# Joint small instructions in a token-major norm, gates spread differently, and sums of logarithms as fp32r products, in a two-block transformer kernel

## The chip, the cores and the metric

The kernel runs on one core of one Trainium2 chip. The metric is device time in microseconds (us) from launch to end, the median of three runs. One further execution was recorded by the hardware profiler; its trace is what the prediction is argued from. Engines are named as in the profile: PE (matrix products), PEld (its weight loads), DVE (vector), ACT (scalar), POOL (GpSimd), SP (which here only issues DMAs).

## The reference, cut to what matters

A first block (four mixers, a feed-forward layer with squared ReLU, a gated per-layer embedding) is followed by two DeepNorm layers. Layer 0 is dilated attention and a sparse mixture of 16 experts, layer 1 is stick-breaking attention and the same kind of mixture. There are 256 tokens of 1024 features, all in float32. The parts that the change touches:

```python
def rmsnorm(x, g):                 # before the feed-forward layer, the gates and the dilated attention
    y = x32 * lax.rsqrt(jnp.mean(x32 * x32, axis=-1, keepdims=True) + EPS)

def layer_norm(x, g, b):           # after each mixture: x = layer_norm(ALPHA * x + ffn, ...)
    mu = xf.mean(-1, keepdims=True)
    var = jnp.square(xf - mu).mean(-1, keepdims=True)
    return ((xf - mu) * lax.rsqrt(var + LN_EPS) * g + b).astype(x.dtype)

# stick-breaking attention, per head; z is the clipped score
sp = jnp.where(strict, jnp.log1p(jnp.exp(z)), 0.0)      # the logarithms
r_in = jnp.einsum('bhnqj,js->bhnqs', sp, suffix)        # their sums from key j on
att = jnp.where(strict, jnp.exp(z - r_in), 0.0)
```

## The kernel before, in words

Tokens lie along the free dimension (256 columns), features along the partitions in eight blocks of 128. A weight piece (1024x256) comes by DMA on SP's queue as `raw` tiles of 128x1024; ACT casts each to fp32r (`whi`) and DVE takes the rest (`wlo`, raw minus whi). An activation is split in the same way (`s` tiles, `sp.hi` and `sp.lo`). A product is then three fp32r matmuls (whi·hi, wlo·hi, whi·lo), `mm3`. There are four `whi` and four `wlo` tiles, so two pieces at a time; SP's next DMA waits for a tile to come free. The remaining products (`sc<-half,ones`, `sc<-sbl,consts`) are plain fp32, which the PE runs as two passes each; the trace counts each pass as a matmul. All `mm` calls have line L250, all `tt` L239, `stt` L247, `act` L236, so tiles tell them apart.

The order on each engine is set by a list scheduler over the program; each engine then runs its own list in order. Stages on the trace's clock: mixers to 330, feed-forward 331 to 518, gates to 548, dilated attention 548 to 800, first mixture 850 to 985, stick-breaking attention 994.5 to 1107, second mixture 1139 to 1275, last norm and output to 1290.7.

What the change touches:

- `rstd` (L432) squares eight blocks in four ACT passes of 128x512, adds the first three (`tot`) and leaves `[tot, sq]`. Each holds two blocks, so four fp32 products with `ones` sum over partitions; with `halve` the two halves of each tile are added first and two products are left. `late` (in the feed-forward, and again at the gates) and `dilated`'s `ev_q` call it without `halve`, the mixers with it.
- `proj_beside` (L406) multiplies the first query and the first key piece of an attention side by side, each block in the order whi·hi, wlo·hi, whi·lo. `stick`'s `begin` is its second caller.
- `stick` (L1335) has four quads of heads, two head pairs each, two heads in a pair: 16 score tiles `z`. Per tile, `scores` makes `l` (`sbl`), `sums` multiplies it by `suffix` (128x384) and `ones` (128x128) into `sc`.
- `token_norm` (L1812) normalises a mixture's result with tokens on partitions (two tiles of 128 tokens, each in two column halves of 512). After layer 0 `across_norm` transposes the result back for `stick`, after 32 products that only keep the PE busy (`warm`); after layer 1 it applies gain and shift (`along`) and issues the output DMAs.

Of the kernel before, what the change touches and what calls it, by code (L numbers as in the profile page):

```python
# [8 lines left out]
F32 = mybir.dt.float32  # L9
F32R = mybir.dt.float32r  # L10
BF = mybir.dt.bfloat16
I32 = mybir.dt.int32
AF = mybir.ActivationFunctionType
OP = mybir.AluOpType
AX = mybir.AxisListType

D = 1024
S = 256
# [185 lines left out]
class Kern:  # L204
# [141 lines left out]

    def piece(self, n=1, beside=None):

        while len(self.made) < n + 1 and self.pieces:
            src, width = self.pieces.pop(0)  # L350
            self.made.append(self.wsplit(src, width, beside=beside))
            beside = None
        now, self.made = self.made[:n], self.made[n:]
        return now if n > 1 else now[0]

    @staticmethod
    def cut(parts, o, n):
# [45 lines left out]
                             x, lambda t: t[:, k], k == 0, k == kt - 1)  # L403
            evac(j, p.rearrange("p (b t) -> p b t", b=2))

    def proj_beside(self, ws, kt, x, evacs, step):  # L406


        out = [self.ps() for _ in ws]
        for k0 in range(0, kt, step):  # L410
            for w, p in zip(ws, out):
                for b in range(2):
                    for k in range(k0, min(k0 + step, kt)):
                        self.mm3(p[:, b * S:(b + 1) * S], w, k * S + b * 128, 128,
                                 x, lambda t: t[:, k], k == 0 and b == 0, k == kt - 1)
        for p, evac in zip(out, evacs):
            evac(0, p.rearrange("p (b t) -> p b t", b=2))
# [14 lines left out]
    def rstd(self, x, nb, eps, dim, halve=False):  # L432

        p = self.ps(next(t for t in ("sc", "acc", "ps") if t in self.banks))
        tot = None
        for b in range(0, nb - nb % 2, 2):
            sq = self.half()
            self.act(sq, x[:, b:b + 2], AF.Square)
            if tot is None:
                tot = sq  # L440
            elif b < nb - 2:
                self.tt(tot, tot, sq, OP.add)
        both = [tot] if tot is sq else [tot, sq]
        if halve:
            for t in both:
                self.tt(t[:, 0], t[:, 0], t[:, 1], OP.add)
        terms = [t[:, i] for t in both for i in range(1 if halve else 2)]
        if nb % 2:
            sq = self.row()
            self.act(sq, x[:, nb - 1], AF.Square)  # L450
            terms.append(sq)
        for i, t in enumerate(terms):
            self.mm(p[:, :S], self.ones, t, i == 0, i == len(terms) - 1)
        r = self.X.tile([128, S], F32, name="rstd", bufs=2)
        self.act(r, p[:, :S], AF.Sqrt, scale=1.0 / dim, bias=self.eps[eps])
        self.nc.vector.reciprocal(r, r)
        return r
# [362 lines left out]
    def first_tail(self, acc):  # L820
        nc, A, ap = self.nc, self.A, self.ap
        x = self.x2()
# [17 lines left out]

        def late():
            if not rs:
                rs.append(self.rstd(x, 8, 1e-6, D))
            return rs[0]
        accp = [self.ps("acc") for _ in range(4)]

# [327 lines left out]
    def dilated(self, x, h):  # L1174
# [12 lines left out]
        def ev_q(quad, g):  # L1187
            def ev(j, p):
                nonlocal r
                if r is None:  # L1190
                    r = self.rstd(x, 8, 1e-6, D)
                    self.table("natural_log_exp_and_others")
                tiles["q", quad, g] = heads("dq")
                self.stt(tiles["q", quad, g], p, 0.125, self.bc2(r), OP.mult, OP.mult)
            return ev
# [139 lines left out]
    def stick(self, x, h):  # L1335
        nc, A, ap = self.nc, self.A, self.ap
        self.table("natural_log_exp_and_others")
        self.later_pieces()
        at = self.new_split(8)
        tiles = {}  # L1340

        def ev(n, quad, scale):
            def evac(j, p):
# [3 lines left out]

        def begin():
            self.proj_beside(self.piece(2), 8, h,
                             [ev("q", 0, 0.125), ev("k", 0, 1.0)], 2)  # L1350

        def query(quad):
            self.proj(self.piece(), 8, 2, h, ev("q", quad, 0.125))
# [7 lines left out]
        def scores(quad, hp):  # L1361

            q, k = tiles["q", quad], tiles["k", quad]
            ps = [self.ps("sc") for _ in range(2)]
            for c in range(2):
                for s, p in enumerate(ps):
                    r = slice(64 * s, 64 * s + 64)
                    self.mm(p[:, c * S:384 - 128 * (1 - c)], k[r, hp, c * 128:c * 128 + 128], q[r, hp, c * 128:],
                            True, True)
            zs = [A.tile([128, 384], F32, name="sbz", bufs=6) for _ in ps]  # L1370
            ls = [A.tile([128, 384], F32, name="sbl", bufs=6) for _ in ps]
            for p, z in zip(ps, zs):
                self.ts(z, p[:, :384], 60.0, OP.min, -60.0, OP.max)
            for z, l in zip(zs, ls):
                self.act(l, z, AF.Abs)
                self.act(l, l, AF.Exp, scale=-1.0)
                self.act(l, l, AF.Ln, bias=1.0)
                self.stt(l, z, 0.0, l, OP.max, OP.add)
                for c in (0, 256):
                    self.tt(l[:, c:c + 128], l[:, c:c + 128], self.k["strict_t"], OP.mult)  # L1380
            tiles["z", quad, hp] = zs, ls

        def sums(quad, hp):

            for z, l in zip(*tiles["z", quad, hp]):
                pr = self.ps("sc")
                self.mm(pr[:, :384], self.k["suffix"], l, True, False)
                self.mm(pr[:, 128:256], self.ones, l[:, 256:384], False, True)
                self.tt(z, z, pr[:, :384], OP.subtract)
                self.act(z, z, AF.Exp)  # L1390
                for c in (0, 256):
                    self.tt(z[:, c:c + 128], z[:, c:c + 128], self.k["strict_t"], OP.mult)
# [231 lines left out]
    def moe(self, layer, x):  # L1624
# [113 lines left out]
            nc.vector.tensor_copy(hs, pt[:, :2 * n].rearrange("p (b t) -> p b t", b=2))  # L1738
            return hs

        def down(i, hs):


            yparts.append(yparts.pop(0))
            y = yparts[0]
            wd = wsp[1] if i == 8 else self.beside([ap["e_d"][layer, 2 * i + s] for s in range(2)], 2048)
            for n in range(2):
                p = self.ps("y")
                c = slice(n * 512, n * 512 + 512)
                for k in range(1 if i == 8 else 2):  # L1750
                    for s in range(2):
                        if i == 8:
                            l, r, last = hs[:, s], wd[s][:, c], True
                        else:
                            l, r, last = hs[:, k, 64 * s:64 * s + 64], wd[s][k][:, c], k == 1
                        self.mm(p[64 * s:64 * s + 64], l, r, k == 0, last)
                self.act(y[:, 0, c], p, AF.Copy)
                self.tt(y[:, 1, c], p, y[:, 0, c], OP.subtract)
            return y
# [22 lines left out]
        for n, i in enumerate(order):  # L1782
# [17 lines left out]
            with self.behind(*self.last_mm):  # L1800
                prev = i, hidden(i, p)
        self.raws, self.turn = raws, -1
        across(7)
        back(*ys.pop(0), False, False)
        y = down(*prev)
        self.table("sqrt_and_others")
        along2 = [along("rows2", k) for k in range(2)] if layer else None
        self.S16.reverse()
# [3 lines left out]
    def token_norm(self, layer, xr, acc, along):  # L1812
# [5 lines left out]
        for n, c in enumerate(cols):  # L1818
            for t in range(2):
                nc.vector.tensor_tensor_reduce(xr[:, t, c], xr[:, t, c], acc[t][n], 1.0, 0.0, OP.add, OP.add,  # L1820
                                               accum_out=sums[:, t, n:n + 1])
                sq = self.half().rearrange("p b t -> p (b t)")
                self.act(sq, xr[:, t, c], AF.Square, accum_out=sqs[:, t, n:n + 1])
        for t in range(2):
            o = slice(t, t + 1)
            self.tt(nm[:, o], sums[:, t, 0:1], sums[:, t, 1:2], OP.add)
            self.tt(rs[:, o], sqs[:, t, 0:1], sqs[:, t, 1:2], OP.add)
            self.ts(nm[:, o], nm[:, o], -1.0 / D, OP.mult)
            self.tt(u[:, o], nm[:, o], nm[:, o], OP.mult)
            self.stt(rs[:, o], rs[:, o], 1.0 / D, u[:, o], OP.mult, OP.subtract)  # L1830
            self.act(rs[:, o], rs[:, o], AF.Sqrt, bias=self.eps[1e-5])
            nc.vector.reciprocal(rs[:, o], rs[:, o])
            self.tt(nmr[:, o], nm[:, o], rs[:, o], OP.mult)
            for n, c in enumerate(cols):
                if n:
                    self.ts(xr[:, t, c], xr[:, t, c], rs[:, o], OP.mult, nmr[:, o], OP.add)
                else:
                    self.act(xr[:, t, c], xr[:, t, c], AF.Identity, scale=rs[:, o], bias=nmr[:, o])
                if along:
                    self.tt(xr[:, t, c], xr[:, t, c], along[0][:, c], OP.mult)  # L1840
                    self.tt(xr[:, t, c], xr[:, t, c], along[1][:, c], OP.add)
                    nc.sync.dma_start(self.out[t * 128:t * 128 + 128, c], xr[:, t, c])

    def across_norm(self, xr, layer):

# [62 lines left out]
    def tail(self, x, dense):  # L1908
# [6 lines left out]
        with self.phase("moe0" + n, **banks):  # L1915
# [11 lines left out]
            else:  # L1927
                x, sp = self.across_norm(self.rest, 0)
            self.dbg("ln2" + n, x)
        with self.phase("sb" + n):  # L1930
            self.stick(x, sp)
        with self.phase("moe1" + n, **banks):
            moe(1, x)
            if dense:
# [62 lines left out]
```

## Time and profile before

| | |
|---|---|
| median of three runs | 1289.57 us (1289.53, 1289.57, 1291.12) |
| profiled execution | 1292.46 us, its span 1290.7 us |
| PE busy | 1258.6 us (98%) |
| DVE, ACT busy | 731.3 us (57%), 610.2 us (47%) |
| mean granted PE clock | 0.991 of full speed |

A row of the timeline gives start, busy time, engine, line, operation, out<-in, shapes and the number of instructions joined in it; matmuls overlap, so the pace of PE is read from one row's start to the next one's, not from the busy time. The bracket at the end is the engine's idle time before the row and what ended it.

### The profile page before, as it was taken

To read this page: it belongs to the slowest core of one execution; us is meant where nothing else is said; L and a number is where in the kernel's file an instruction comes from. 1 tells how busy PE (TensorE), PEld (TensorE's weight loads), DVE (VectorE), ACT (ScalarE), POOL (GpSimd) and SP (SyncE) were. 2 spreads that over 40 slices of the span, in tenths; PEclk is the share of its full clock that TensorE was granted. 3 is DMA by queue.
4 is the path that set the end of the run, shared out by engine and by line. 5 is a ranking of instruction groups with operands and counts; after the bars stand their busy time and mean duration, and the time that the engine had idled before them with its cause. 6 is when DMAs were issued, how large, how long until landed. Compare 5 with 4: busy or idle time off the path is not lost.

```text
span 1290.7 us, 22672 instructions
## 1 busy us (share of the span) xinstructions
PE 1258.6 (98%) x9159; PEld 1043.3 (81%) x9159; DVE 731.3 (57%) x1416; ACT 610.2 (47%) x951; POOL 24.8 (2%) x48
## 2 busy tenths in 40 slices
PE   9999999999999999999999999999998999999995
PEld 7987899999999999999999999855334999754332
DVE  7877667558665545876464646263215677454214
ACT  6674666446544544755454545232115666242112
POOL 0000000000000000000000000002000000002000
PEclk9999999999999999999999999999999999999998
DMA  7452346657486555566464645599999444557893
GB/s 263 147 183 71 109 137 204 187 178 241 142 300 229 178 186 176 185 190 187 141 194 134 194 134 170 166 318 332 358 395 370 131 131 131 191 196 272 331 397 132
DMA packets 91105, 268.28 MB, mean 208 GB/s; under 512 B 26528, under 2 KB 26672, under 8 KB 90736
## 3 DMA queue, kind: packets, MB, share of 16 engines
q1 hardware_dynamic: 86576, 252.80, 58.5%
q0 software_dynamic: 4416, 13.94, 3.2%
q8 instruction: 74, 1.21, 0.4%
q14 instruction: 39, 0.32, 0.1%
HBM read 267.68 MB, written 6.89 MB: 213 GB/s over the span
## 4 chain that ended last, share of the span: by engine, by line
PE 86%; DVE 5%; DMA 4%; ACT 3%; issue 1%; SPq 0%; ACTq 0%; DVEq 0%
PE ps L250 54%; PE acc L250 14%; PE y L250 6%; PE sc L250 4%; PE o L250 2%; PE sd L250 1%; PE o L258 1%; ACT whi L236 1%; DVE wlo L239 1%; PE sc L1265 1%; DMA raw<-e_d 1%; PE tr L250 1%; DMA s<-rows 1%; DMA wlo<-e_gu 1%; DMA raw<-e_gu 1%
## 5 line engine op out<-in xcount | busy, mean ns | idle before, releaser
L250 PE MATMUL ps<-s,whi 128*128 128x256 f32 x2656 | 495.0, 286 | 5.3 <-DVE s L239 2.5
L239 DVE TENSOR_TENSOR wlo<-raw,whi 128x1024 fp32r<-128x1024 f32 x276 | 333.8, 1218 | 258.5 <-ACT whi L236 258.0
L236 ACT ACTIVATE whi<-raw 128x1024 fp32r<-128x1024 f32 x276 | 287.1, 1054 | 307.1 <-PE ps L250 222.9
L250 PEld LDWEIGHTS ps<-s,whi 128*128 128x128 f32 x2656 | 414.9, 190 | 12.3 <-DVE s L239 4.0
L250 PE MATMUL ps<-s,wlo 128*128 128x256 f32 x1328 | 378.2, 285 | 1.3 <-DVE wlo L239 1.3
L250 PEld LDWEIGHTS ps<-s,wlo 128*128 128x128 f32 x1328 | 251.0, 189 | 4.6 <-DVE wlo L239 2.6
L250 PE MATMUL acc<-hid,whi 128*128 128x256 f32 x512 | 93.0, 281 | 0.0
L250 PE MATMUL ps<-whi,s 128*128 128x256 f32 x512 | 92.3, 282 | 0.0
L250 PE MATMUL ps<-raw,xg 128*64 128x512 f32 x344 | 86.2, 597 | 0.0
L250 PEld LDWEIGHTS ps<-whi,s 128*128 128x128 f32 x512 | 78.2, 188 | 1.5
L250 PEld LDWEIGHTS acc<-hid,whi 128*128 128x128 f32 x512 | 79.3, 189 | 0.0
L250 PE MATMUL acc<-hid,wlo 128*128 128x256 f32 x256 | 72.3, 283 | 0.0
L250 PE MATMUL ps<-wlo,s 128*128 128x256 f32 x256 | 71.7, 280 | 0.0
L250 PEld LDWEIGHTS ps<-raw,xg 128*64 128x64 f32 x344 | 25.7, 136 | 43.9 <-issue 40.5
L236 ACT ACTIVATE eh<-ps 128x256 f32<-128x256 f32 x16 | 6.2, 385 | 114.9 <-PE ps L250 114.9
L247 DVE SCALAR_TENSOR_TENSOR eh<-ps,gslot,eh 128x256 f32<-128x256 f32 x16 | 7.7, 484 | 85.2 <-ACT eh L236 85.2
L236 ACT ACTIVATE s<-y 128x512 fp32r<-128x512 f32 x36 | 21.0, 597 | 69.2 <-PE y L250 69.2
L239 DVE TENSOR_TENSOR s<-y,s 128x512 fp32r<-128x512 f32 x36 | 24.3, 686 | 50.6 <-ACT s L236 50.4
L250 PEld LDWEIGHTS ps<-wlo,s 128*128 128x128 f32 x256 | 48.1, 188 | 0.0
L250 PE MATMUL acc<-s,whi 128*128 128x256 f32 x256 | 47.7, 286 | 0.3 <-ACT dprobT L236 0.3
L250 PEld LDWEIGHTS acc<-hid,wlo 128*128 128x128 f32 x256 | 47.9, 187 | 0.0
L250 PE MATMUL y<-raw,hs 128*64 128x512 f32 x180 | 46.7, 600 | 0.0
(407 smaller groups left out, 1748.9 us busy)
## 6 DMA issues: line engine op xcount, KB each, us to landing
raw<-e_gu SPq DMA_DIRECT2D x81, 512.0 KB, 7.9
raw<-w_dil SPq DMA_DIRECT2D x72, 512.0 KB, 4.6
raw<-w_ff SPq DMA_DIRECT2D x64, 512.0 KB, 4.7
raw<-e_d SPq DMA_DIRECT2D x43, 512.0 KB, 10.1
raw<-w_g SPq DMA_DIRECT2D x32, 512.0 KB, 4.0
whi<-e_gu SPq DMA_DIRECT2D x31, 512.0 KB, 8.4
raw<-w_a SPq DMA_DIRECT2D x28, 512.0 KB, 4.8
raw<-w_sb SPq DMA_DIRECT2D x24, 512.0 KB, 7.8
```

The lines of the kernel that those rows point to most:

```text
L236: return self.nc.scalar.activation(out, in_, func, **k)
L239: return self.nc.vector.tensor_tensor(out, a, b, op=op)
L247: return self.nc.vector.scalar_tensor_tensor(out, a, s, b, op0=op0, op1=op1, **k)
L250: self.last_mm = self.nc.tensor.matmul(out, l, r, start=first, stop=last, skip_group_check=True).ins,
L258: self.nc.tensor.matmul(p, self.ones_b, r, start=True, stop=True, skip_group_check=True)
L1265: nc.tensor.transpose(pt[:, c * 128:(c + 1) * 128], e[:, order[c]], self.k["ident"])
```

## The change

Five edits. (1) `rstd` with `halve` first adds its two tiles into one, so one product is left, and all three calls without `halve` now have it. (2) `proj_beside` can put all products with `x.hi` first and those with `x.lo` at the end; `stick` asks for that. (3) `token_norm` takes both token tiles in each small instruction, and with gain and shift uses four `stt` for each of two fused passes: (x - mean)·gain, then ·rstd + shift. (4) `stick` splits `l` into an fp32r pair and multiplies `suffix` and `ones`, cast once to fp32r, by both. (5) Calls in the mixture stand in another order: the last expert's down weights and the preparation of stick's pieces, and `nhalf` is 3 instead of 4 in `stick`. The DMA lists of SP and of POOL are the same before and after, instruction by instruction.

```diff
-    def proj_beside(self, ws, kt, x, evacs, step):
+    def proj_beside(self, ws, kt, x, evacs, step, second=False):
         out = [self.ps() for _ in ws]
-        for k0 in range(0, kt, step):
+        for part in (0, 1) if second else ():
+            for k0 in range(0, kt, step):
+                for w, p in zip(ws, out):
+                    for b in range(2):
+                        for k in range(k0, min(k0 + step, kt)):
+                            for i, xp in ((0, x.lo),) if part else ((0, x.hi), (1, x.hi)):
+                                self.mm(p[:, b * S:(b + 1) * S], self.cut(w[i], k * S + b * 128, 128), xp[:, k],
+                                        not part and i == 0 and k == 0 and b == 0, part == 1 and k == kt - 1)
+        for k0 in () if second else range(0, kt, step):
...
         if halve:
-            for t in both:
-                self.tt(t[:, 0], t[:, 0], t[:, 1], OP.add)
+            if len(both) > 1:
+                self.tt(tot, tot, both.pop(), OP.add)
+            self.tt(tot[:, 0], tot[:, 0], tot[:, 1], OP.add)
...
-                rs.append(self.rstd(x, 8, 1e-6, D))
+                rs.append(self.rstd(x, 8, 1e-6, D, True))
...
-                    r = self.rstd(x, 8, 1e-6, D)
+                    r = self.rstd(x, 8, 1e-6, D, True)
...
+        suffix, ones = (A.tile([128, 128], F32R, name=n) for n in ("suffix_r", "ones_r"))
+        nc.vector.tensor_copy(suffix, self.k["suffix"])
+        nc.vector.tensor_copy(ones, self.ones)
...
-                             [ev("q", 0, 0.125), ev("k", 0, 1.0)], 2)
+                             [ev("q", 0, 0.125), ev("k", 0, 1.0)], 2, True)
...
-            ls = [A.tile([128, 384], F32, name="sbl", bufs=6) for _ in ps]
+            parts = [[A.tile([128, 384], F32R, name=n, bufs=4) for n in ("sblh", "sbll")] for _ in ps]
+            ls = [A.tile([128, 384], F32, name="sbl", bufs=2) for _ in ps]
...
+                self.act(hi, l, AF.Copy)
+                self.tt(lo, l, hi, OP.subtract)
+            tiles["z", quad, hp] = zs, parts
...
-                self.mm(pr[:, :384], self.k["suffix"], l, True, False)
-                self.mm(pr[:, 128:256], self.ones, l[:, 256:384], False, True)
+                for i, l in enumerate(parts):
+                    self.mm(pr[:, :384], suffix, l, i == 0, False)
+                    self.mm(pr[:, 128:256], ones, l[:, 256:384], False, i == 1)
...
+        wd = down_weights(prev[0])
+        if not layer:
+            self.later_pieces()
+            self.make(0)
...
+        self.tt(nm, sums[:, :, 0], sums[:, :, 1], OP.add)
+        self.ts(nm, nm, -1.0 / D, OP.mult)
+        def centre(t):
+            for c in cols:
+                self.stt(xr[:, t, c], xr[:, t, c], nm[:, t:t + 1], along[0][:, c], OP.add, OP.mult)
+        if along:
+            centre(0)
+        self.tt(u, nm, nm, OP.mult)
+        self.tt(rs, sqs[:, :, 0], sqs[:, :, 1], OP.add)
+        self.stt(rs, rs, 1.0 / D, u, OP.mult, OP.subtract)
+        self.act(rs, rs, AF.Sqrt, bias=self.eps[1e-5])
+        if along:
+            centre(1)
+        nc.vector.reciprocal(rs, rs)
...
+                if along:
+                    self.stt(xr[:, t, c], xr[:, t, c], rs[:, o], along[1][:, c], OP.mult, OP.add)
+                    nc.sync.dma_start(self.out[t * 128:t * 128 + 128, c], xr[:, t, c])
```

On PE, where `stick` begins, the kernel before has the transposes of the normed tokens and then the 96 products of the first pieces, the whi·lo product of each block standing between the others (`s_10704` is the split input, hi and lo in one name):

```order
L1853 MATMUL y<-consts,x_9682 128x128 x4
L1853 MATMUL ps<-consts,x_9682 128x128 x2
L1853 MATMUL tr<-consts,x_9682 128x128 x2
L250 MATMUL ps<-s_10704,whi 128x256 x2
L250 MATMUL ps<-s_10704,wlo 128x256
L250 MATMUL ps<-s_10704,whi 128x256 x2
L250 MATMUL ps<-s_10704,wlo 128x256
```

On PE at the end of that step the changed kernel has this (the input is `s_10692` there); the last three rows are the value projection:

```order
L250 MATMUL ps<-s_10692,whi 128x256
L250 MATMUL ps<-s_10692,wlo 128x256
L250 MATMUL ps<-s_10692,whi 128x256
L250 MATMUL ps<-s_10692,wlo 128x256
L250 MATMUL ps<-s_10692,whi 128x256 x32
L250 MATMUL ps<-whi,s_10692 128x256 x2
L250 MATMUL ps<-wlo,s_10692 128x256
L250 MATMUL ps<-whi,s_10692 128x256 x2
```

The 32 products with the low part have moved from between the others to the end of the step, so 64 products stand ahead of the first one that reads a low part.

On PE in `sums`, before, for the two heads of a pair:

```order
L250 MATMUL ps<-s_10704,wlo 128x256
L250 MATMUL sc<-sbl,consts 128x384
L250 MATMUL sc<-sbl,ones 128x128
L250 MATMUL sc<-sbl,consts 128x384
L250 MATMUL sc<-sbl,ones 128x128
```

and in the changed kernel:

```order
L250 MATMUL ps<-s_10692,wlo 128x256
L250 MATMUL sc<-sblh,suffix_r 128x384
L250 MATMUL sc<-sblh,ones_r 128x128
L250 MATMUL sc<-sbll,suffix_r 128x384
L250 MATMUL sc<-sbll,ones_r 128x128
```

Two fp32 products (two passes each) for one tile have become four fp32r products of one pass.

On DVE in the last norm, before (`x_12315` is the result in tokens, `s_12907` gain and shift):

```order
L1832 RECIPROCAL tn_r<-tn_r 128x1
L239 TENSOR_TENSOR tn_b<-tn_m,tn_r 128x1
L244 TENSOR_SCALAR x_12315<-x_12315,tn_r,tn_b 128x512
L1832 RECIPROCAL tn_r<-tn_r 128x1
L239 TENSOR_TENSOR x_12315<-x_12315,s_12907 128x512 x4
L239 TENSOR_TENSOR tn_b<-tn_m,tn_r 128x1
L244 TENSOR_SCALAR x_12315<-x_12315,tn_r,tn_b 128x512
L239 TENSOR_TENSOR x_12315<-x_12315,s_12907 128x512 x4
```

and in the changed kernel:

```order
L239 TENSOR_TENSOR tn_m<-tn_s 128x2
L243 TENSOR_SCALAR tn_m<-tn_m 128x2
L247 SCALAR_TENSOR_TENSOR x_12403<-x_12403,tn_m,s_12995 128x512 x2
L239 TENSOR_TENSOR tn_u<-tn_m 128x2
L239 TENSOR_TENSOR tn_r<-tn_q 128x2
L247 SCALAR_TENSOR_TENSOR x_12403<-x_12403,tn_m,s_12995 128x512
L247 SCALAR_TENSOR_TENSOR tn_r<-tn_r,tn_u 128x2
L247 SCALAR_TENSOR_TENSOR x_12403<-x_12403,tn_m,s_12995 128x512
L1865 RECIPROCAL tn_r<-tn_r 128x2
L247 SCALAR_TENSOR_TENSOR x_12403<-x_12403,tn_r,s_12995 128x512 x4
```

Ten wide DVE instructions (and two on ACT, not shown) have become eight, and four of these stand ahead of the reciprocal.

## Rows read from the trace of the kernel before

**Rows 1.** The page: PE's busy time, and the chain by engine.

```profile
PE 1258.6 (98%) x9159; PEld 1043.3 (81%) x9159; DVE 731.3 (57%) x1416; ACT 610.2 (47%) x951; POOL 24.8 (2%) x48
PE 86%; DVE 5%; DMA 4%; ACT 3%; issue 1%; SPq 0%; ACTq 0%; DVEq 0%
```

**Rows 2.** Chain of waits (start us, us, what): rstd's products at gates and dilated attention.

```profile
529.31 1.73 PE acc L250 x8
560.46 1.73 PE sc L250 x8
```

**Rows 3.** Timeline: rstd in the feed-forward (PE), gates and dilated attention (DVE).

```profile
331.18 1.03 PE L250 MATMUL acc<-half,ones 128*128 128x256 f32 x4
...
531.59 1.75 DVE L456 RECIPROCAL rstd<-rstd 128x256 f32<-128x256 f32 x1
...
555.96 1.48 DVE L239 TENSOR_TENSOR half<-half 128x512 f32<-128x512 f32 x2
```

**Rows 4.** Timeline: the start of stick, PE, ACT and DVE.

```profile
994.51 0.38 PE L250 MATMUL ps<-s,whi 128*128 128x256 f32 x1
...
996.08 0.39 PE L250 MATMUL ps<-s,whi 128*128 128x256 f32 x1 [1.19 <-DVE s L239]
...
997.84 0.55 PE L250 MATMUL ps<-s,whi 128*128 128x256 f32 x1 [1.14 <-DVE s L239]
...
998.81 0.83 ACT L236 ACTIVATE s<-ps,vecs 128x256 fp32r<-128x256 f32 x1 [1.53 <-DVE x L244]
...
1003.37 1.06 ACT L236 ACTIVATE whi<-raw 128x1024 fp32r<-128x1024 f32 x1 [1.86 <-PE ps L250]
...
1010.37 0.28 PE L250 MATMUL ps<-s,wlo 128*128 128x256 f32 x1
...
1012.21 0.92 PE L250 MATMUL sc<-dq,dk 64*128 64x256 f32 x8
```

**Rows 5.** Windows (busy us by engine, PEclk, DMA share, GB/s): the start of stick.

```profile
998.00:1001.00 3.00, 3.00 (x15) 3.00 (x16) 2.91 (x8) 2.18 (x3) 0.00 (x0) 0.50 0.04 18
1002.00:1010.00 8.00, 8.00 (x69) 8.00 (x68) 2.56 (x3) 3.00 (x3) 0.00 (x0) 1.00 0.33 97
```

**Rows 6.** Chain of waits: the second quad of stick, products of sums among projections.

```profile
1042.65 5.95 PE ps L250 x48
1048.60 1.73 PE sc L250 x8
1050.34 5.76 PE ps L250 x48
1056.10 1.73 PE sc L250 x8
```

**Rows 7.** Timeline, PE and PEld: fp32r products of 320 columns, weight loads for 32 columns.

```profile
1178.47 1.33 PE L250 MATMUL y<-oneh,s 128*128 128x320 f32 x8
1179.65 0.75 PE L250 MATMUL tr<-oneh,s 128*128 128x320 f32 x4
...
1181.26 0.67 PEld L250 LDWEIGHTS tr<-r_gparts,oneh 128*128 128x128 f32 x6
```

**Rows 8.** Timeline: DVE's last mask of a score pair; windows: a stretch of stick.

```profile
1047.61 0.49 DVE L239 TENSOR_TENSOR sbl<-sbl,consts 128x128 f32<-128x128 f32 x2
...
1000.00:1050.00 50.00, 49.97 (x395) 46.49 (x395) 34.26 (x66) 33.19 (x53) 0.00 (x0) 0.99 0.41 127
```

**Rows 9.** Timeline: the last norm, DVE; and the same kind of fused pass earlier.

```profile
910.63 2.50 DVE L247 SCALAR_TENSOR_TENSOR x<-s,x 128x512 f32<-128x512 f32 x4 [6.56 <-DMA s<-rows]
...
1277.04 0.28 DVE L239 TENSOR_TENSOR tn_m<-tn_s 128x1 f32<-128x1 f32 x2
...
1282.45 2.50 DVE L239 TENSOR_TENSOR x<-x,s 128x512 f32<-128x512 f32 x4
```

**Rows 10.** The second mixture's end: windows, then the chain of waits.

```profile
1225.00:1262.00 37.00, 36.60 (x158) 14.26 (x154) 4.83 (x10) 4.50 (x10) 0.00 (x0) 1.00 1.01 393
...
1226.73 9.54 DMA raw<-e_gu
```

More of the change, by code (lines that the diff above doesn't have):

```diff
@@ L347, in piece, with make @@
     def piece(self, n=1, beside=None):
-        while len(self.made) < n + 1 and self.pieces:
+        self.make(n + 1, beside)
+        now, self.made = self.made[:n], self.made[n:]
+        return now if n > 1 else now[0]
+    def make(self, n, beside=None):
+        while len(self.made) < n and self.pieces:
             src, width = self.pieces.pop(0)
@@ L352, in piece @@
             beside = None
-        now, self.made = self.made[:n], self.made[n:]
-        return now if n > 1 else now[0]
     @staticmethod
@@ L1337, in stick @@
         self.table("natural_log_exp_and_others")
-        self.later_pieces()
+        if self.dense:
+            self.later_pieces()
         at = self.new_split(8)
         tiles = {}
+        suffix, ones = (A.tile([128, 128], F32R, name=n) for n in ("suffix_r", "ones_r"))
+        nc.vector.tensor_copy(suffix, self.k["suffix"])
+        nc.vector.tensor_copy(ones, self.ones)
         def ev(n, quad, scale):
@@ L1370, in scores @@
             zs = [A.tile([128, 384], F32, name="sbz", bufs=6) for _ in ps]
-            ls = [A.tile([128, 384], F32, name="sbl", bufs=6) for _ in ps]
+            parts = [[A.tile([128, 384], F32R, name=n, bufs=4) for n in ("sblh", "sbll")] for _ in ps]
+            ls = [A.tile([128, 384], F32, name="sbl", bufs=2) for _ in ps]
             for p, z in zip(ps, zs):
                 self.ts(z, p[:, :384], 60.0, OP.min, -60.0, OP.max)
-            for z, l in zip(zs, ls):
+            for z, l, (hi, lo) in zip(zs, ls, parts):
                 self.act(l, z, AF.Abs)
@@ L1380, in scores @@
                     self.tt(l[:, c:c + 128], l[:, c:c + 128], self.k["strict_t"], OP.mult)
-            tiles["z", quad, hp] = zs, ls
+                self.act(hi, l, AF.Copy)
+                self.tt(lo, l, hi, OP.subtract)
+            tiles["z", quad, hp] = zs, parts
         def sums(quad, hp):
-            for z, l in zip(*tiles["z", quad, hp]):
+            for z, parts in zip(*tiles["z", quad, hp]):
                 pr = self.ps("sc")
-                self.mm(pr[:, :384], self.k["suffix"], l, True, False)
-                self.mm(pr[:, 128:256], self.ones, l[:, 256:384], False, True)
+                for i, l in enumerate(parts):
+                    self.mm(pr[:, :384], suffix, l, i == 0, False)
+                    self.mm(pr[:, 128:256], ones, l[:, 256:384], False, i == 1)
                 self.tt(z, z, pr[:, :384], OP.subtract)
@@ L1739, in hidden, with down_weights, down @@
             return hs
-        def down(i, hs):
+        def down_weights(i):
+            return wsp[1] if i == 8 else self.beside([ap["e_d"][layer, 2 * i + s] for s in range(2)], 2048)
+        def down(i, hs, wd=None):
             yparts.append(yparts.pop(0))
             y = yparts[0]
-            wd = wsp[1] if i == 8 else self.beside([ap["e_d"][layer, 2 * i + s] for s in range(2)], 2048)
+            wd = wd or down_weights(i)
             for n in range(2):
@@ L1802, in moe @@
         self.raws, self.turn = raws, -1
+        wd = down_weights(prev[0])
+        if not layer:
+            self.later_pieces()
+            self.make(0)
         across(7)
         back(*ys.pop(0), False, False)
-        y = down(*prev)
+        y = down(*prev, wd)
         self.table("sqrt_and_others")
@@ L1823, in token_norm @@
                 self.act(sq, xr[:, t, c], AF.Square, accum_out=sqs[:, t, n:n + 1])
+        self.tt(nm, sums[:, :, 0], sums[:, :, 1], OP.add)
[12 more added lines that the diff above has]
+        nc.vector.reciprocal(rs, rs)
+        if not along:
+            self.tt(nmr, nm, rs, OP.mult)
         for t in range(2):
             o = slice(t, t + 1)
[L1826 to L1833, printed above, removed]
             for n, c in enumerate(cols):
-                if n:
+                if along:
+                    self.stt(xr[:, t, c], xr[:, t, c], rs[:, o], along[1][:, c], OP.mult, OP.add)
+                    nc.sync.dma_start(self.out[t * 128:t * 128 + 128, c], xr[:, t, c])
+                elif n:
                     self.ts(xr[:, t, c], xr[:, t, c], rs[:, o], OP.mult, nmr[:, o], OP.add)
@@ L1838, in token_norm @@
                     self.act(xr[:, t, c], xr[:, t, c], AF.Identity, scale=rs[:, o], bias=nmr[:, o])
[L1839 to L1842, printed above, removed]
     def across_norm(self, xr, layer):
@@ L1929, in tail @@
             self.dbg("ln2" + n, x)
+        self.nhalf = 3
         with self.phase("sb" + n):
             self.stick(x, sp)
+        self.nhalf = 4
         with self.phase("moe1" + n, **banks):
```

## The prediction

> **What bounds the kernel now.** I read the page first: PE is busy 98% of the span and is 86% of the chain of waits [rows 1]. So an edit is worth what it takes from PE's list, or from a place where PE waits, or from the tail after PE's last product; work on ACT and DVE counts only where PE or the end waits for it. Next the chain by stage, for the products named in the diff: rstd's eight passes stand in the chain whole at the gates and in the dilated attention [rows 2], the products of `sums` at each head pair of stick [rows 6]. Then the timeline of the only stage start that the diff reorders [rows 4], with the granted clock there [rows 5], and the timeline of the last norm, where only DVE, ACT and the output DMAs work [rows 9]. Last the windows of the second mixture, which follows most of the edits and in which DMA is busy throughout near the end [rows 10].
>
> **rstd.** Three calls go from four fp32 products to one. Eight passes take 1.73 [rows 2], so a product takes 1.73 / 4 = 0.43, three take 1.30, and three places 3.9. The row at 331.18 shows the same products in the feed-forward, in two groups [rows 3]. Each call gains two DVE adds, 128x512 and 128x256, for which 1.48 / 2 = 0.74 each is an upper bound [rows 3]. DVE's reciprocal takes 1.75 there while PE goes on with other products [rows 3], which shows that r is not waited for at once; I cost the adds at nothing, and if they were on the path the loss would be 3 x 1.5 = 4.4, which undoes this term. I take 3.8, range -0.6 to 3.9. The mixers lose one more product of 0.43 where DVE sets the pace; nothing is counted.
>
> **The start of stick.** Today PE starts its first product at 994.51, waits 1.19 and 1.14 for DVE's low parts, and then has a stretch at half the granted clock: 0.50 at 998 to 1001, where 15 products start in 3.0 us, against 69 in 8.0 at 1.00 [rows 4, 5]. The 96 products end at 1010.37 + 0.12 = 1010.5; at 8.0 / 69 = 0.116 to 0.12 each they are worth 11.5. In the new order the first 64 wait only for ACT's high parts. ACT works through them steadily except for one, whose start at 998.81 followed 1.53 of waiting for DVE [rows 4]; it ends at 999.6. Starting at 994.7, PE has done 33 products of the first blocks by about 998.9, waits some 0.7 there, and does the other 31 by 1003.3; the 32 low ones end at 1007.2, gain 3.3. Part is given back: the four `whi` tiles of the two first pieces are now read until the end of the step. ACT's cast into the first freed tile stood at 1003.37 [rows 4]; it becomes about 1005, the second one about 1006.9 to 1007.9, and dq and dk, which stand behind both on ACT's list, follow at 0.6 each, so dk is there at about 1009. PE reaches the first score products (1012.21 now, [rows 4]) after six value products, 1008.0, and waits about 0.9. Net 2.6. The norm ahead of it (joint 128x2 instructions) shortens DVE's list there but puts one more `wlo` in front of the last scale; I take 0.2 off: 2.4. Bounds: 0 if the waits only change names, 4.3 if neither the 0.7 nor the 0.9 appears.
>
> **The sums.** Sixteen tiles; a pair costs 1.73 today [rows 6], a tile 0.865. After: two fp32r products of 384 columns and two of 128. fp32r takes 5.76 / 48 = 0.12 at 256 columns [rows 6] and (1179.65 - 1178.47) / 8 = 0.147 at 320 [rows 7], so 0.174 at 384, going on in a line. No fp32r product between 32 and 256 columns is in the trace. Six of 32 columns have their weight loads in 0.67, 0.11 each [rows 7], and 256 columns take 0.12; if the price rises with the columns, 128 columns cost 0.115. The other end is that fp32r at 128 columns costs as much as today's whole fp32 product: shared out by columns, 0.865 x 128 / 512 = 0.216. So a tile takes 2 x 0.174 + 2 x 0.115 = 0.578, saving 0.287, or 0.780, saving 0.085: 4.6 or 1.4 in all. I take 4.6, as the nearest fp32r rows lie on both sides in columns and both at the lower price.
>
> The Trainium skill bears on that price twice (TensorE: Matmul & The Clock Gate). Its section on the back-to-back issue gap gives columns / 2.4 + 2.5 ns, which is 56 ns at 128 columns and would make the sums worth 6.5; its section on LDWEIGHTS gives 107 ns to load 128 columns of weights, by which no product here is cheaper than that. The rows side with the second: 0.11 per weight load with 32 columns to multiply [rows 7].
>
> What hides the split of `l`: each tile gains one ACT copy and one DVE subtraction of 128x384. Upper bounds are the cast of 128x1024, 1.06 [rows 4], and a fused pass of 128x512, 2.50 / 4 = 0.63 [rows 9]. In a quad of 24.3 us ACT is busy 33.19 / 50 and DVE 34.26 / 50 of the time [rows 8], 16.1 and 16.7; with four more each that is at most 20.4 and 19.2. The last mask of a pair ends at 1048.1 [rows 8] and its products come at 1056.10 [rows 6]: 8 us of slack for a detour of at most 2.2. The other side is ACT's list: the copies wait for DVE's masks and the next `whi` stands behind them. A piece of weights is needed one piece (5.76) later than the one in work [rows 6], so a delay of 1 to 2 us is covered. Cost 0.
>
> **The last norm.** Today from 1277.04 DVE has small instructions, two scales, and two groups of four 128x512 passes, the last from 1282.45 to 1284.95 [rows 9]. After: eight fused passes at 2.50 / 4 = 0.625 [rows 9], 5.0, and about 0.8 of small ones, four passes running while ACT finishes its squares and root: 1277.04 + 5.8 = 1282.9. Gain 2.0, range 1.0 (the root is waited for) to 2.3; the output DMAs follow each pass as today.
>
> **The rest.** The moved calls and `nhalf` change no DMA's place on SP's or POOL's list: 0. Sum: 3.8 + 2.4 + 4.6 + 2.0 = 12.8. It is made in the profiled execution, 1292.46 with a span of 1290.7, where the runs' median is 1289.57; these differ by 0.2%, far less than the terms, so I take the sum from the median: 1276.8.
>
> **Rivals.**
> A. fp32r at 128 columns runs at the upper price. For it: only columns far from 128 are in the trace. Sums 1.4, total 9.6: 1280.0.
> B. The half clock stays. For it: PE's products before it, nine between 994.5 and 998, were sparse, and the new order still has thin places; against: 33 products now come at once. 3 us at 0.50 cost 1.5: 1278.3. The Trainium skill (TensorE: Matmul & The Clock Gate, HAM oscillation) has waits between groups of products put the engine back to its low rate, and the trace's 0.50 behind two waits agrees.
> C. DMA takes stick's gains back. DMA is busy 1.01 of the time at 1225 to 1262 and the chain runs through `e_gu` for 9.54 at 1226.73 [rows 10]. Against: the DMAs wait for tiles that PE and DVE release, so they start earlier when PE does. It would cost 2.4 + 4.6: 1283.8.
> D. Slower: on ACT's list in stick the copy of `l` waits for DVE, and `whi` behind it comes late. It decides once PE waits over 12.8 / 8 = 1.6 at each of eight score steps; at 2.0 each the time is 1289.6 + 3.2 = 1292.8. Against it stands the slack of 5.76.
> E. The change does not do what it says in sum: rstd's adds cost what its products save, and C holds. 12.8 - 4.4 - 7.0 = 1.4 of gain: 1288.2.
>
> **Numbers.** Forecast 0.42, A 0.30, B 0.11, C 0.09, E 0.04, D 0.04. A measurement of this kernel tells 0.2%, 2.6 us, from no change. Faster is forecast, A, B and C: 0.92; the same E: 0.04; slower D: 0.04. The range takes in A, B and C and a little beyond C; its low end has the upper bounds of the start, the norm and rstd and the mixers' product, 1.9 + 0.3 + 0.1 + 0.4 = 2.7, below the forecast: 1274 to 1285.
>
> **What would show it.** rstd: two passes of `half,ones` at each of three places and no DVE idle before the next split. Stick: the first 64 products with waits of under 1 us in sum and PEclk 1.00 from 998; a wait for dk before the first score products. Sums: a pair in 1.16 (A: 1.56) and a quad 1.1 shorter. Last norm: DVE's last pass ends 5.9 after the first small instruction, where it is 7.9 now. I am wrong if the second mixture takes longer than before by what stick saved, or if PE's waits in stick grow.

## The result, and the profile after

The changed kernel takes 1277.38 us (1276.45 to 1278.32, 4 runs), the kernel before beside it 1290.09: ratio 0.9901 (95% interval 0.9883 to 0.9918). A second set gave 1277.18 against 1289.49, 0.9905 (0.9891 to 0.9919). Forecast was 1276.8. Ratios below are to the kernel before, each with its interval.

The spans of the two profiled executions, 1290.7 and 1274.4, differ by more, 16.3. So I compare by stretch, each measured from a start to a start in one profile:

| stretch | before | after | shorter by | forecast |
|---|---|---|---|---|
| feed-forward, to the gates' product with `ones` | 222.64 | 221.37 | 1.27 | 1.3 |
| gates, to the dilated attention's product with `ones` | 31.14 | 31.05 | 0.09 | 1.3 |
| from there to the first score product | 25.07 | 23.77 | 1.30 | 1.3 |
| norm and transposes ahead of stick | 9.81 | 10.17 | -0.36 | -0.2 |
| start of stick, to the second query | 23.76 | 20.82 | 2.94 | 2.6 |
| from there to the next experts' squares (all sums) | 99.76 | 95.05 | 4.71 | 4.6 |
| last norm, DVE's first pass to the end of its last | 10.34 | 8.81 | 1.53 | 2.0 |

Together 11.48 of the forecast 12.8. The other 4.8 of the spans' difference are 1.64 in the mixers and 1.7 in each mixture, less 0.2 in the rest of the dilated attention; mixers and mixtures scatter between executions of the same code (below).

The start of stick, in the timeline after [rows 4]:

```profile
989.07 0.39 PE L250 MATMUL ps<-s,whi 128*128 128x256 f32 x1 [0.24 <-ACT s L236]
...
990.77 0.39 PE L250 MATMUL ps<-s,whi 128*128 128x256 f32 x1 [1.20 <-ACT s L236]
...
1003.01 0.92 PE L250 MATMUL sc<-dq,dk 64*128 64x256 f32 x8
```

and the same stretch in the windows of after (PEclk is third from the end), against 0.50 and 1.00 in [rows 5]:

```profile
989.00:1002.00 13.00, 11.73 (x95) 11.53 (x96) 8.47 (x17) 7.60 (x12) 0.00 (x0) 1.00 0.24 95
```

There is one wait of 1.20 for ACT instead of two for DVE, no stretch at the low clock, and no wait over 0.15 ahead of the scores. The sums in the chain of after, answering [rows 6]:

```profile
1033.12 5.95 PE ps L250 x48
1039.06 1.10 PE sc L250 x8
1040.16 5.80 PE ps L250 x48
1045.96 1.09 PE sc L250 x8
```

In the chain a pair costs 1.10 instead of 1.73, where 1.16 was forecast. Read from start to start the two pairs of a quad take 1.10 and 1.18, before 1.65 and 1.83: 0.60 less on average, and eight of them make the 4.7 of the table. In the timeline of after, part of one such pair:

```profile
1038.90 0.34 PE L250 MATMUL sc<-sblh,suffix_r 128*128 128x384 f32 x1
1039.08 0.22 PE L250 MATMUL sc<-sblh,ones_r 128*128 128x128 f32 x1
1039.14 0.39 PE L250 MATMUL sc<-sbll,suffix_r 128*128 128x384 f32 x1
1039.36 0.22 PE L250 MATMUL sc<-sbll,ones_r 128*128 128x128 f32 x1
1039.42 0.39 PE L250 MATMUL sc<-sblh,suffix_r 128*128 128x384 f32 x1
```

From start to start the 128 columns take 0.06 and the 384 after them 0.22, where the first 384 take 0.18: 0.28 for the two. PEld's rows bear on why the second 384 take longer:

```profile
1039.08 0.19 PEld L250 LDWEIGHTS sc<-sbll,suffix_r 128*128 128x128 f32 x1
1039.19 0.19 PEld L250 LDWEIGHTS sc<-sbll,ones_r 128*128 128x128 f32 x1
```

The load of their weights starts with the short product ahead of them, at 1039.08, and the next load starts 0.11 later, when the long product has been going for 0.05. The gates, in the chain of after [rows 2]:

```profile
526.40 0.43 PE acc L250 x2
526.83 15.75 PE ps L250 x132
542.58 1.19 DVE s L247 x3
543.77 1.18 DVE wlo L239
544.95 0.61 DVE half L239
545.56 0.14 issue
545.70 11.76 PE ps L250 x96
557.46 0.43 PE sc L250 x2
```

The two groups of products are 1.30 shorter each. The chain leaves PE for DVE between them, as it does before; how long PE itself stands idle there the timelines tell, first of the kernel before, then of after:

```profile
550.21 0.38 PE L250 MATMUL ps<-s,whi 128*128 128x256 f32 x1 [0.34 <-DVE s L247]
```
```profile
545.70 0.47 PE L250 MATMUL ps<-s,whi 128*128 128x256 f32 x2 [1.59 <-DVE half L239]
```

Last, DVE in the last norm of after [rows 9]:

```profile
1262.84 1.41 DVE L247 SCALAR_TENSOR_TENSOR x<-x,tn_m,s 128x512 f32<-128x512 f32 x2
1264.17 0.15 DVE L239 TENSOR_TENSOR tn_u<-tn_m 128x2 f32<-128x2 f32 x1
1264.24 0.15 DVE L239 TENSOR_TENSOR tn_r<-tn_q 128x2 f32<-128x2 f32 x1
1264.31 0.74 DVE L247 SCALAR_TENSOR_TENSOR x<-x,tn_m,s 128x512 f32<-128x512 f32 x1
...
1265.90 2.74 DVE L247 SCALAR_TENSOR_TENSOR x<-x,tn_r,s 128x512 f32<-128x512 f32 x4
```

A fused pass (two operations of DVE in one instruction) takes 2.74 / 4 = 0.685, not the 0.625 of [rows 9].

### The profile page after: what moved, and what is told of

The parts are those of the page before. It is cut to its first block, busy times and chain, and to the rows that moved or that the text cites. A ratio compares the mean times of both kernels' runs of the same rounds, so it can differ in the third digit from the quotient of the medians.

```text
span 1274.4 us, 22651 instructions
## 1 busy us (share of the span) xinstructions
PE 1244.7 (98%) x9139; PEld 1035.7 (81%) x9139; DVE 738.2 (58%) x1423; ACT 613.4 (48%) x963; POOL 24.8 (2%) x48
## 4 chain that ended last, share of the span: by engine, by line
PE 87%; DVE 4%; DMA 4%; ACT 3%; issue 1%; SPq 0%; DVEq 0%; ACTq 0%
PE ps L250 55%; PE acc L250 14%; PE y L250 6%; PE sc L250 4%; PE o L250 2%; PE sd L250 1%; PE o L258 1%; PE sc L1277 1%; DVE wlo L239 1%; ACT whi L236 1%; DMA raw<-e_d 1%; PE tr L250 1%; DMA wlo<-e_gu 1%; DMA raw<-e_gu 1%; DMA raw<-w_sb 1%
```

## The experiments

The first four take one part each out of the changed kernel.

**rstd.** Both calls back to `self.rstd(x, 8, 1e-6, D)`.

> The changed kernel, with the feed-forward's, the gates' and the dilated attention's rstd back at four products each. Theory (the nine fp32 products removed were on PE's path, 0.43 each, and the DVE adds are hidden): 3.9 us longer than the changed kernel, 1281.3. Rival (the adds cost what the products saved): no longer, 1277.4.

Measured 1282.35, ratio 0.9941 (0.9927 to 0.9955): slower than the changed kernel, by 4.6 at 0.9905, with intervals of 1.8 on either side. By stretches: feed-forward 222.65, gates 31.14, dilated 25.07, so 1.28 + 0.09 + 1.30 = 2.7; the rest of the 4.6 lies within the intervals. The rival falls; the theory holds for two places of three.

**Start of stick.** `proj_beside(..., 2, True)` back to `2`.

> The changed kernel, with the first pieces of stick multiplied in the old order. Theory (PE waited for DVE's low parts and then ran at the low clock): 2.4 to 2.9 us longer, about 1280.1, with the two waits for DVE and a stretch of granted clock 0.50 back in the first 7 us of stick. Rival (the start is set by the norm ahead of it): 1277.4, same waits as the changed kernel.

Measured 1282.11, 0.9936 (0.9923 to 0.995). The stretch takes 24.84 against 20.82. Timeline and window of this kernel:

```profile
990.97 0.38 PE L250 MATMUL ps<-s,whi 128*128 128x256 f32 x1 [1.20 <-DVE s L239]
...
992.73 0.58 PE L250 MATMUL ps<-s,whi 128*128 128x256 f32 x1 [1.14 <-DVE s L239]
```
```profile
992.00:998.00 6.00, 5.27 (x24) 5.27 (x25) 4.87 (x11) 2.83 (x4) 0.00 (x0) 0.50 0.08 33
```

Both waits and the low clock are back, the clock here for the whole 6 us of the window instead of the 3 of [rows 5], and the step loses 4.0 instead of 2.9. The rival falls, and rival B of the prediction with it.

**Sums.** `sums` and `scores` as before.

> The changed kernel, with the sums of logarithms as fp32 products and no split of the logarithms. Theory (a pair 1.73 instead of 1.09, eight pairs, ACT and DVE hidden): 5.1 us at most, 4.7 by the trace's milestones, longer: 1282.1. Rival (DMA in the second mixture takes the gain back): under 2 us longer, below 1279.4.

Measured 1283.41, 0.9948 (0.9935 to 0.9962), 5.5 slower at 0.9905. Pairs cost 1.73 again; the stretch is 99.75 against 95.05. The second mixture took 135.59, inside its scatter, so DMA did not take the gain back: rival C falls.

**Norms.** `token_norm` as before.

> The changed kernel, with the old token-major norm at both places. Theory: 1.5 us for the last norm as the two traces show, less 0.4 that the joint instructions lose ahead of stick: 1.1 longer, 1278.5. Rival (as predicted, 2.0 less 0.2): 1279.2.

Measured 1279.8, 0.9922 (0.9909 to 0.9936), 2.2 slower at 0.9905, which does not tell 1.1 from 2.0. The stretches do: last norm 10.34 against 8.81, ahead of stick 9.80 against 10.17.

**Moved calls alone**, put into the kernel before:

```diff
+        wd = down_weights(prev[0])
+        if not layer:
+            self.later_pieces()
+            self.make(0)
         across(7)
...
-        y = down(*prev)
+        y = down(*prev, wd)
```

> The kernel before, with the moved calls alone (down weights of the last expert, preparation of stick's pieces, nhalf 3 in stick). Theory (no DMA changes its place, the 1.7 us by which each mixture was shorter in the profile of the changed kernel are scatter of the DMAs between executions): 1290, no change. Rival (the moved calls shorten each mixture by 1.7): 1286.6.

Measured 1289.87 (11 runs) against 1290.79 (14 runs), 0.9994 (0.9984 to 1.0005): no change. Its mixtures take 133.49 and 135.56. Over all profiles the first takes 132.7 to 134.6 and the second 134.0 to 136.0, with the change and without it.

**ACT's order.** The high products of stick's start in the order in which ACT makes the blocks:

```diff
-            for k0 in range(0, kt, step):
+            for k0 in range(0, kt, step) if part else (0, 2, 4, 1, 3, 6, 5, 7):
...
-                        for k in range(k0, min(k0 + step, kt)):
+                        for k in range(k0, min(k0 + step, kt) if part else k0 + 1):
```

> The changed kernel, with the high products of stick's first pieces in the order in which ACT delivers the blocks (0, 2, 4, 1, 3, 6, 5, 7), one block at a time. Theory (PE's wait of 1.20 is for block 1, which ACT makes fourth): the wait goes, the step ends 1.2 to 1.4 earlier, 1276.1. Rival (the wait returns at the next late block, or as a wait for the value's weights): 1277.4.

Measured 1278.37, 0.9912 (0.9897 to 0.9926); once more beside the changed kernel:

> The changed kernel with the high products of stick's first pieces in ACT's order, once more beside the changed kernel. Theory (the stage was 1.46 shorter): 1.4 under the changed kernel of the same chip. Rival (the gain is lost in the second mixture's DMAs): the same as the changed kernel.

1277.1 (1275.24 to 1277.71, 4 runs), 0.9902 (0.9887 to 0.9917), with the changed kernel at 0.9905. In the timeline PE no longer waits behind its first product:

```profile
990.93 0.39 PE L250 MATMUL ps<-s,whi 128*128 128x256 f32 x1 [0.24 <-ACT s L236]
991.16 0.28 PE L250 MATMUL ps<-s,wlo 128*128 128x256 f32 x1
991.28 0.28 PE L250 MATMUL ps<-s,whi 128*128 128x256 f32 x1
```

The stretch is 19.37 in both profiles, 1.45 shorter than 20.82. So the wait was for block 1, fourth on ACT's list; that the whole kernel gains from it the times don't settle, since 1.45 lies within their intervals.

**Constants in the last passes.** `0.001` for `nm[:, t:t + 1]` and `0.999` for `rs[:, o]`.

> The changed kernel, with constants (0.001 and 0.999) in place of the per-token mean and scale in the eight last passes, which leaves that part of the last norm out. Theory (a per-partition scalar makes a 128x512 fused pass 0.06 longer than a constant does): the passes go from 0.685 to 0.625 each, the last ends 0.5 earlier after the first sum than in the changed kernel. Rival (the passes are longer because the output DMAs and ACT read the same tile): they stay at 0.685.

The timeline of its one execution:

```profile
1265.83 0.68 DVE L247 SCALAR_TENSOR_TENSOR x<-x,s 128x512 f32<-128x512 f32 x1
1266.43 0.15 DVE L239 TENSOR_TENSOR tn_u<-tn_m 128x2 f32<-128x2 f32 x1
...
1267.85 1.87 DVE L247 SCALAR_TENSOR_TENSOR x<-x,s 128x512 f32<-128x512 f32 x3
```

1.87 / 3 = 0.62 and 0.60 from start to start, with ACT and the DMAs on the same tile as before. The theory holds. The norm takes 7.75 instead of 8.81; half of that is order (the first pass no longer waits for the mean).

**32 columns with `ones`.** `pr[:, 128:160]` and `l[:, 256:288]`.

> The changed kernel, with 32 instead of 128 columns in the products with ones, which leaves three quarters of the second block's sums out. Theory (an fp32r product of 128 columns or fewer costs its weight load, 0.11): a pair stays at 1.09. Rival (it costs by its columns): four products of 0.11 lose three quarters, a pair falls to about 0.76.

The timeline of its one execution:

```profile
1041.50 0.18 PE L250 MATMUL sc<-sblh,ones_r 128*128 128x32 f32 x1
1041.53 0.42 PE L250 MATMUL sc<-sbll,suffix_r 128*128 128x384 f32 x1
1041.78 0.18 PE L250 MATMUL sc<-sbll,ones_r 128*128 128x32 f32 x1
1041.81 0.43 PE L250 MATMUL sc<-sblh,suffix_r 128*128 128x384 f32 x1
```

In the chain a pair costs 1.05. The short product falls from 0.06 to 0.03, and the long one behind it grows from 0.22 to 0.25, 0.28 for the two as before: the weights of the long one are not there sooner. The rival (0.76) falls.

**Gates alone.** `halve` off in the gates' call only.

> The changed kernel, with the gates' rstd alone back at four products. Theory (the 1.30 us that its three products took is now spent by PE in a wait of 1.6 to 1.9 for DVE ahead of the dilated attention): same time as the changed kernel; in the profile the time from the gates' first product with ones to the first score product of the dilated attention stays within 0.2 us of 54.8. Rival (the products were on the path as forecast): 1.3 longer, 56.1.

Measured 1278.75, 0.9915 (0.9901 to 0.9929). The gates' stretch is 32.35, 1.30 more; with the next one, 56.1: the rival's number. My theory falls. The wait is there even with the gates' four products back, in this kernel's timeline:

```profile
548.38 0.48 PE L250 MATMUL ps<-s,whi 128*128 128x256 f32 x2 [1.60 <-DVE half L239]
```

So the gates' products were on the path and were saved; another edit made the wait longer, and the stretch 32.35 - 31.14 = 1.21 longer with it. All kernels so far with the wait of 1.6 have the feed-forward's call changed; those without that edit (before, moved calls alone, rstd taken back) wait 0.34. The compiled programs name the place. PE's results go to numbered banks of its output memory (PSUM), and by the program a product that begins a new result in a bank waits until the last one there has been read. The dilated attention's first projection writes bank 0 in the kernel before, the changed one, the one with rstd taken back and this one. The last gate writes bank 2 in the kernel before and with rstd taken back, but bank 0 in the changed kernel and in this one. Compiled with the feed-forward's call alone taken back, the changed kernel has the last gate on bank 2 again; that kernel was not timed.

**PSUM banks.** On top of ACT's order:

```diff
         with self.psum(name, ps=3, sc=4, o=1):
+            for tag in ("sc",) * 4 + ("o",):
+                self.ps(tag)
```

> The kernel of the run before this one, with the PSUM banks of both attentions handed out in another order, so that their first projections take banks that the stage before has long left. Theory (PE's wait at the start of the dilated attention is for the bank that the last gate holds until DVE has read it): the wait of 1.6 for DVE goes, the stretch from the gates' product with ones to the first score product falls by 1.0 to 1.6 from 54.8, and the time with it. Rival (PE waits for the last gate's result itself): the wait moves by a few products and the stretch stays at 54.8.

Measured 1284.83, 0.9958 (0.9945 to 0.9972): slower. At the gates the theory holds. The chain there:

```profile
544.69 0.60 DVE half L239
545.29 0.40 DVE s L247
545.69 0.04 issue
545.74 10.25 PE ps L250 x83
555.99 0.43 PE sc L250 x2
```

The stretch is 29.88 against 31.05, 1.17 shorter. But the same lines hand out stick's banks, and there its first projection got the ones that hold the transposed tokens:

```profile
996.75 0.55 PE L250 MATMUL ps<-s,whi 128*128 128x256 f32 x1 [6.25 <-DVE x L244]
```

That is 6.25 of waiting, and 0.50 of the clock behind it again. The gain at the gates is lost even earlier, at the end of the dilated attention:

```profile
798.28 0.51 PE L250 MATMUL acc<-s,whi 128*128 128x256 f32 x2 [2.00 <-ACT dprobT L236]
```

The same wait is 0.25 in the kernel with ACT's order alone, and from the first score product on the attention takes 1.4 longer than there. An order of banks that changes the hand-over at the gates and nothing else was not tried.

**The changed kernel again.**

> The changed kernel once more, to stand beside the other runs on the same chip. Theory (terms by the profiles' stages: rstd 2.6, start of stick 2.9, sums 4.7, norms 1.2, so 11.4; the rest of the 12.7 measured is scatter of the granted clock in the mixers and of the mixtures' DMAs): 11.4 to 12.0 under the kernel before. Rival (the change also makes the low clock in the mixers rarer): 12.7 again.

1277.18 against 1289.49: 12.3, between theory and rival, with an interval (0.9891 to 0.9919) that holds both. What scatters is seen in one window of it and of the first profile of the same code:

```profile
68.00:72.00 4.00, 4.00 (x20) 3.01 (x20) 3.47 (x8) 1.57 (x4) 0.00 (x0) 0.57 0.54 175
```
```profile
68.00:72.00 4.00, 4.00 (x33) 3.53 (x33) 3.75 (x8) 2.95 (x6) 0.26 (x2) 1.00 0.50 164
```

The first has its granted clock at 0.57 in these 4 us, and its feed-forward comes 1.6 later. Of 12 profiles with the changed rstd in the mixers 4 show the low stretch, and so do both with the old one, too few to say that the change makes it rarer.

## Why the prediction was right, point by point

- **The number.** The stages account for 11.5 of the forecast 12.8: rstd and the norms gave less than forecast, the start of stick a little more. The runs moved by 12.7 and 12.3, with intervals of some 2 us on either side, so they don't tell 11.5 from 12.8. That the measured time lies 0.6 from the forecast is in part luck.
- **Bound.** Right, but for the gates: what left PE's list left the time. The moved calls gave nothing, as counted.
- **rstd.** The price is right (0.43 a product), and so is "I cost the adds at nothing": the feed-forward and the start of the dilated attention gave 1.27 and 1.30 of 1.30. The step that failed is "three places 3.9". I asked whether r was waited for, and not what PE meets next at the gates. There its wait for the last gate's bank grew from 0.34 to 1.59, which took back 1.21 of the 1.30. That it is a bank, the PSUM experiment shows; that the feed-forward's edit moved it follows from the compiled programs, and no timed run changed that call alone.
- **Start of stick.** 2.94 for 2.6, partly by luck, as two errors have opposite signs: the wait was 1.20 at block 1 and not 0.7 later, since I took ACT's blocks to come in the order of their numbers; and PE, held up by that wait, found dk ready, which came 13.9 after the step's first product and not 14.5, as ACT's second cast started earlier than I had it. The sum has a slip, too: 3.3 less 0.9 is 2.4 and not 2.6. That the low clock goes with the waits was right; rival B's nine products ahead of it are five in the timeline, as the count of nine takes in transposes.
- **Sums.** 4.7 for 4.6. Rival A falls: 128 columns did not cost 0.216. But 0.115 is not the product's own time: it takes 0.06, and part of the rest falls on the next product, whose weights are still being loaded. The Trainium skill (TensorE: Matmul & The Clock Gate) has both halves, 56 ns for a product by itself in its section on the back-to-back issue gap and 107 ns in that on LDWEIGHTS. The trace agrees with both: the short product takes 0.06 from start to start, and the loads at 1039.08 and 1039.19 start 0.11 apart.
- **Last norm.** 1.53 for 2.0. The mis-sized term is the pass: 0.685 with a scalar per partition, where the row I took had a constant. Eight times 0.06 are the missing 0.5, and the run with constants shows it.
- **C, D, E.** No gain was lost in the second mixture, which in the two profiles of the changed kernel took 1.7 and 1.1 less than before. PE's waits in stick did not grow: past the start of stick none is over 0.1.

## What to carry to other kernels

When a product leaves a busy engine's list, look for the next hand-over of buffers on that engine, banks included; an edit far upstream can change which bank a stage starts on. Put an engine's work in the order in which its supplier delivers, read from the supplier's own list. For an unmeasured shape, check which operand form the nearest row has, and compare stretches between fixed points: those of the table repeat to 0.1 us from kernel to kernel where no edit touches them, while whole runs scatter by 2 and more.

## What the runs showed of the hardware

- A short fp32r product and a long one behind it cost 0.28 together, whether the short one has 128 or 32 columns: the load of the long one's weights starts with the short product and takes 0.11.
- A 128x512 fused pass on DVE takes 0.06 us more with a scalar per partition than with a constant.
- The granted clock fell to one half for some 3 us at 68 to 72 us in some executions of one kernel and not in others, some 1.6 us of its time.
